# Value products behind the next pair's second score, and the second FFN pass's scale and first weights ahead of the last down products

## The chip, the cores and the metric

The kernel runs on one core of a Trainium2 chip. The core has a tensor engine for matmuls (PE, whose weight loads the profile lists as PEld), a vector engine (DVE), a scalar engine (ACT), a general engine (POOL) and a queue engine (SP, listed as SPq), each with its own queue of instructions; 16 DMA engines move data between HBM, SBUF and so on. Matmul results go to PSUM, which is used here as eight banks of 128 x 512 float32. The metric is the device time of one execution in microseconds; the time before is the median of three runs.

## The reference

One layer of a diffusion backbone on 128 context tokens and 1,024 latent tokens, nine blocks of 128 tokens (block 0 is the context), model width 1,024. Cut to what matters:

```python
h = rmsnorm(x, norm1_w) * (1 + sc1) + sh1
aq, ak, av, mq, mk, mv, mo, mg = split(h @ w_in)
attn_o = attention(aq, keys, vals)          # 8 query heads of 64, 2 key heads; 1,152 keys for latent tokens
hm = mlstm_bidir(...)                       # 4 heads of 128, chunks of 128, forward and backward
x = x + g1 * (concat([attn_o, hm]) @ w_out)
h2 = rmsnorm(x, norm2_w) * (1 + sc2) + sh2
g, u = split(h2 @ w_gu)                     # 2 x 2,816 columns
x = x + g2 * ((silu(g) * u) @ w_down)
y = rmsnorm(x, final_norm_w)
```

Everything is float32. The kernel gets that precision by splitting an operand in a high and a low part and adding three matmuls (high by high, high by low, low by high).

## The kernel before, in words

**Order.** The program is traced by Python generators that hand over to each other; a list scheduler then puts the traced instructions into the engines' queues when the kernel is built. It keeps a timeline of its own, and of the instructions that are ready on it takes the one traced first. `hot(n)` lets a block count as traced n instructions earlier. `tc.issue_after(ins)` queues what its block traces on the engine of `ins` behind `ins`: an order on that one engine, no wait for a result. On the chip each engine then works through its queue in that order. `weave(main, side, n_main, n_side)` (L66) traces `n_side / n_main` units of the side work for each unit of the main work.

**Attention** (L1087). A generator works block by block, head by head. For a head, six matmuls write the scores against all keys into S (L1128), which fills three PSUM banks and has one buffer; DVE takes the maximum (L1130), ACT the exponential (L1131), ACT and DVE make the high and low half-precision parts ph and pl (L1134, L1135), and two DMA transposes on SP's queue turn them into phT and plT (L1137, L1138), which have two buffers each, one for a pair of heads. The value products (L1152, L1153, 18 matmuls for a latent block) of a pair are a closure kept in `late`; it is traced after the second score of the next pair (L1140), or at the end of a group of three blocks (L1165). The last pair of a block is thus traced behind the second score of the next block. ACT and DVE evacuate the result (L1155, L1157). The generator is woven into three stages: beside the mLSTM heads' projections and scans (the first 560 us), beside the output projection and second norm (`prefill`), and beside the first three groups of FFN tiles.

**FFN, first pass.** Blocks 0 to 2 go through an ordinary FFN. The 22 tiles of 128 hidden columns come in five groups, GROUPS = [(0, 4), (4, 4), (8, 4), (12, 5), (17, 5)]. `gate_up` (L1476) takes for each tile a gate and an up piece of 512 KB: load into a raw tile, cast to the high part on ACT (L174), low part on DVE (L145), the sum of the absolute values on ACT (L178, kept in `wsum`), and 24 matmuls (L1472 to L1474). `down` (L1499) then takes the group's rows of w_down in two halves of 512 columns, each in three pieces for a group of five tiles (two of 512 KB, one of 256 KB), and makes 45 matmuls from them (L1214 to L1216), for block 0 first and then for blocks 1 and 2. All raw tiles of this pass come from two buffers in turn:

```python
    raw_tags = ["iraw1"]
    def raw_tile():
        loaded["raw"] = (loaded.get("raw", -1) + 1) % (2 * len(raw_tags))
        return wp.tile([P, 1024], F32, name=nm("raw"), tag=raw_tags[loaded["raw"] // 2], bufs=2)
```

**FFN, second pass.** Blocks 3 to 8 go through a scheme that needs seven products instead of eight for 2 x 2 blocks. `features6` (L1545) makes its inputs Bt while the last two groups of the first pass run: for each of six blocks two halves are transposed on PE, and for blocks 6 to 8 the sums are formed in T (L1575), a tile with one buffer (tag "S" of the pool sp). It is woven as the side work `feats`: 37 units, of which the last block's halves are units 32 and 33. `weight_scale` (L1537) takes the maximum of `wsum`, has PE transpose it (L124), brings it to a power of two on DVE (L190 to L193) and has PE broadcast it (L204). `weights6` (L1588) loads a gate and an up tile into raw tiles, forms four sums on DVE in a tile of the same tag "S" (L1597 to L1600), and for four pairs of operands the scaled high part on ACT (L1605) and the low part on DVE (L1606), in the pool a4p of seven buffers. `pair6` (L1611) calls it and makes the products (L1619 to L1621).

At the seam of the passes (L1824 to L1847) the order traced is: groups four and five whole, `feats` woven in; the rest of `feats`; `weight_scale`; the pools of the first pass closed, a third and fourth raw buffer added (L1841); then `pair6` for the first tile, which starts with `weights6`.

Of the kernel before, what the change touches and what calls it, by code (L numbers as in the profile page):

```python
# [49 lines left out]
def hybrid_step(ctx: ExitStack, tc: tile.TileContext, I: dict, O: dict):  # L50
# [24 lines left out]
    def emit(gen):  # L75
        for _ in gen:
            pass

    def chain(*gens):
        for g in gens:  # L80
            for v in g:
                yield v
# [1004 lines left out]
    def attention(c, oT, done, ha=200, hv=200, spill=None):  # L1087

        late = []
        for i in range(CB):  # L1090
            b = c * CB + i
            nk = 1 if b == 0 else NB
            with hot(ha):
                qr = ap.tile([P, NQ, HD], F32, name=nm("qr"), tag="qr", bufs=1)
                nc.scalar.dma_start(qr.rearrange("p h d -> p (h d)"), q_d[b])
                qT = ap.tile([P, NQ, P], F32R, name=nm("qT"), tag="qT", bufs=1)
                flat = qr.rearrange("p h d -> p (h d)")
                ps = bank()
                for j in range(4):
                    transpose(ps[:, j * P : (j + 1) * P], flat[:, j * P : (j + 1) * P])  # L1100
                psv = ps.rearrange("p (j x) -> p j x", j=4)
                qv = qT.rearrange("p (j g) x -> p j g x", g=2)
                for g in range(2):
                    own = slice(64 * g, 64 * g + 64)
                    far = slice(64 - 64 * g, 128 - 64 * g)
                    nc.scalar.copy(qv[own, :, g, :], psv[own])
                    sub(qv[far, :, g, :], psv[own], qv[own, :, g, :].bitcast(F32), "dve")
            yield
            for h in range(NQ):
                with hot(ha):  # L1110
                    kv = h // 4
                    if h % 2 == 0:
                        phT = ap2.tile([P, 2, NB, P], F16, name=nm("phT"), tag="phT", bufs=2)
                        plT = ap2.tile([P, 2, NB, P], F16, name=nm("plT"), tag="plT", bufs=2)
                    pr = ap2.tile([P, 3, CT], F32, name=nm("pr"), tag="pr", bufs=2)
                    ph = ap2.tile([P, 3, CT], F16, name=nm("ph"), tag="ph", bufs=2)
                    pl = ap2.tile([P, 3, CT], F16, name=nm("pl"), tag="pl", bufs=2)
                    st = ap.tile([P, 4], F32, name=nm("st"), tag="st", bufs=4)
                    if b == 0:
                        prv, phv, plv = pr[:, 0:1, 0:P], ph[:, 0:1, 0:P], pl[:, 0:1, 0:P]  # L1120
                        parts, w, c0 = 1, P, NB * P
                    else:
                        prv, phv, plv = pr, ph, pl
                        parts, w, c0 = 3, CT, 0
                    S = psum["S"].tile([P, 3, 512], F32, name=nm("S"), tag="S")
                    for n in range(parts):
                        for t in range(2):
                            mm(S[:, n, 0:w], qT[:, h, :], kst[kv][:, t, c0 + n * w : c0 + (n + 1) * w], start=(t == 0), stop=(t == 1))  # L1128
                    Sv = S[:, 0:parts, 0:w]
                    dve.tensor_reduce(out=st[:, 0:1], in_=Sv, axis=AX.XY, op=ALU.max, negate=True)  # L1130
                    act(prv, Sv, AF.Exp, bias=st[:, 0:1], accum_out=st[:, 1:2])  # L1131
                    dve.reciprocal(st[:, 2:3], st[:, 1:2])
                    dve.tensor_scalar(out=st[:, 3:4], in0=st[:, 2:3], scalar1=2.0 ** 14, scalar2=None, op0=ALU.mult)  # L1133
                    act(phv, prv, AF.Copy, scale=st[:, 3:4])  # L1134
                    dve.scalar_tensor_tensor(out=plv, in0=prv, scalar=st[:, 3:4], in1=phv, op0=ALU.mult, op1=ALU.subtract)  # L1135
                    dma_t = nc.sync.dma_start_transpose
                    dma_t(phT[:, h % 2, 0:nk, :], phv.rearrange("p a b -> p (a b)"))  # L1137
                    loaded["turned"] = dma_t(plT[:, h % 2, 0:nk, :], plv.rearrange("p a b -> p (a b)")).ins  # L1138
                yield
                if late and h % 2 == 1:  # L1140
                    late.pop()()
                    yield
                if h % 2 == 1:
                    def values(phT=phT, plT=plT, kv=kv, nk=nk, b=b, i=i, j=h // 2):
                        if j == 0:
                            oT.append(new_oT() if spill is None else ap2.tile([P, 4, P], F32, name=nm("oS"), tag="oS", bufs=1))
                        with hot(hv):
                            po = psum["po"].tile([P, 512], F32, name=nm("po"), tag="po") if "po" in psum else bank()
                            for n in range(nk):
                                vi = 9 if b == 0 else n  # L1150
                                v = vs[:, vi, kv].rearrange("p t d -> p (t d)")
                                mm(po[:, 0:256], v, phT[:, :, n, :], start=(n == 0), stop=False)  # L1152
                                mm(po[:, 0:256], v, plT[:, :, n, :], start=False, stop=(n == nk - 1))  # L1153
                            ol = ap2.tile([64, 256], F32, name=nm("ol"), tag="ol", bufs=1)
                            act(ol, po[64:128, 0:256], AF.Copy, scale=vsc[64:128, 1:2])  # L1155
                            for g in range(2):
                                dve.scalar_tensor_tensor(out=oT[i][64 * g : 64 * g + 64, j, :],  # L1157
                                                         in0=po[0:64, g * P : (g + 1) * P], scalar=vsc[0:64, 1:2],
                                                         in1=ol[:, g * P : (g + 1) * P], op0=ALU.mult, op1=ALU.add)
                        if j == 3:  # L1160
                            done.add(i)
                            if spill is not None:
                                dma(spill[i].rearrange("p (k x) -> p k x", k=4), oT[i])
                    late.append(values)
        late.pop()()  # L1165
        yield
# [443 lines left out]

    def pair6(f, Bt, acts):  # L1611

        ops = weights6(f)
        a, b, c, d = (bank()[:, 0:CT] for _ in range(4))

        def product(n, ps, first):
# [195 lines left out]
    with tc.issue_after(loaded["gate"]):  # L1812
        for _ in range(4):
# [10 lines left out]
    firsts = []  # L1824
    feats = chain(*[features6(nxt, 1, i, Bt, firsts) for i in range(CB)],
                  attn_out(far, o2, g_d[0, 1], lambda i: mixing(a4p, "A4", 7), o_d[CB:]), *[features6(far, 2, i, Bt, firsts) for i in range(CB)])
    main = groups(0, cur, GROUPS[NG:])
    weave(main, feats, 18 * sum(nf for _, nf in GROUPS[NG:]), 42)
    emit(feats)
    weight_scale()  # L1830
    es_f.close()
    es_ps.close()
    del psum["mm1"], psum["po"]
# [78 lines left out]
```

## Time and profile before

| | |
|---|---|
| median of 3 runs | 1542.33 us (1539.0 to 1546.64) |
| the profiled execution's own time | 1538.01 us |
| its span in the profile | 1536.2 us |
| mean granted PE clock | 0.97 |
| PE, DVE, ACT, POOL busy | 93%, 73%, 53%, 14% |

The profile is of one execution. Its views: a page (busy time by engine, slices, DMA, the chain of work that ended last, the costliest groups of instructions); a list of waits (who waited for whom, total us, times, longest); a timeline (start, length, engine, line, output<-inputs, and in brackets the idle time before it and what ended it); groups of instructions by line (count, busy us, mean ns, idle before); and windows (for a stretch A:B its length, then busy us and number of instructions by engine, the granted PE clock, the DMA share and GB/s; a window can be kept to one line of the kernel, and then shows that line's instructions alone). Times are from the start of the span. Matmuls overlap, so that a busy time per matmul is longer than its slot; where a number of matmuls fills a stretch, the stretch divided by the number gives the slot.

### The profile page before, as it was taken

The numbers are of one execution on the slowest core, as the hardware profiler recorded it, in microseconds if no ns is written. First come the engines' busy times: TensorE is split into PE (matmuls) and PEld (weight loads), VectorE is DVE, ScalarE is ACT, GpSimd is POOL, SyncE is SP. The second block draws the span as 40 slices with busy tenths as digits, with TensorE's granted clock in tenths as the row PEclk, the third lists the DMA queues.
The fourth block names the chain that finished last, engine by engine and source line by source line (L and its number), as shares of the span: only waits on it lengthen the run. The fifth ranks groups of instructions, "written<-read, shape, count | busy, mean of one in ns | idle before, by whom it ended". The sixth has DMA issues, their size and how long they took to land.

```text
span 1536.2 us, 22786 instructions
## 1 busy us (share of the span) xinstructions
PE 1434.6 (93%) x8281; PEld 1071.1 (70%) x8281; DVE 1126.6 (73%) x2272; ACT 810.7 (53%) x1524; POOL 222.4 (14%) x310
## 2 busy tenths in 40 slices
PE   6889899899899889999999899989999999999995
PEld 3635567676677657888989787965766667676763
DVE  4978557685777778646787766879878696886857
ACT  4855476676766745552866752844334141523233
POOL 0122332132323344510001010000000000000000
PEclk9799999999999999999999999999999999999997
DMA  9475245565449756564778733444222040412112
GB/s 371 155 227 186 68 90 96 72 150 78 81 102 158 197 187 170 145 206 138 212 177 193 185 117 117 143 132 153 81 72 94 28 137 1 138 49 76 35 35 82
DMA packets 255318, 197.02 MB, mean 128 GB/s; under 512 B 167974, under 2 KB 209142, under 8 KB 255206
## 3 DMA queue, kind: packets, MB, share of 16 engines
q1 hardware_dynamic: 252638, 191.13, 45.9%
q10 hardware_dynamic: 2440, 4.05, 1.2%
q8 instruction: 65, 1.06, 0.3%
q0 software_dynamic: 128, 0.39, 0.1%
q14 instruction: 47, 0.39, 0.1%
HBM read 143.94 MB, written 13.26 MB: 102 GB/s over the span
## 4 chain that ended last, share of the span: by engine, by line
PE 53%; DVE 4%; DMA 4%; ACT 4%; issue 1%; POOL 1%; SPq 0%; ACTq 0%; POOLq 0%
PE mm L1621 7%; PE mm L1619 7%; PE mm L1620 7%; PE mm L1687 4%; PE mm L1688 4%; PE mm L1689 4%; PE mm L1472 3%; PE mm L1474 3%; PE mm L1473 3%; PE mm L1214 2%; PE mm L1216 2%; PE mm L1215 2%; PE mm L1250 2%; DMA raw<-in_w_gu_dram 2%; PE mm L1252 2%; PE mm L1254 1%
## 5 line engine op out<-in xcount | busy, mean ns | idle before, releaser
L1619 PE MATMUL mm<-Bt,A 128*128 128x384 f16 x616 | 200.2, 328 | 1.6 <-ACT A L1605 1.6
L1620 PE MATMUL mm<-Bt,A 128*128 128x384 f16 x616 | 201.6, 327 | 0.0
L1621 PE MATMUL mm<-Bt,A 128*128 128x384 f16 x616 | 197.2, 327 | 2.4 <-DVE A L1606 2.4
L174 ACT CAST whi<-raw 128x1024 fp32r<-128x1024 f32 (+1 forms) x102 | 103.3, 1014 | 132.5 <-DMA raw<-in_w_down_dram 49.0
L145 DVE TENSOR_TENSOR wlo<-raw,whi 128x1024 fp32r<-128x1024 f32 (+1 forms) x102 | 120.7, 1183 | 53.8 <-ACT whi L174 49.0
L1135 DVE SCALAR_TENSOR_TENSOR pl<-pr,st,ph 128x1152 f16<-128x1152 f32 (+1 forms) x72 | 95.7, 1329 | 48.8 <-ACT ph L1134 45.1
L1472 PE MATMUL mm<-aTh,whi 128*128 128x384 f32 x352 | 121.7, 346 | 8.8 <-ACT ol L1155 3.1
L1474 PE MATMUL mm<-aTh,wlo 128*128 128x384 f32 x352 | 120.9, 344 | 0.8 <-DVE wlo L145 0.8
L1473 PE MATMUL mm<-aTl,whi 128*128 128x384 f32 x352 | 120.9, 343 | 0.0
L1130 DVE TENSOR_REDUCE st<-S 128x1 f32<-128x1152 f32 (+1 forms) x72 | 88.9, 1235 | 21.7 <-PE S L1128 21.2
L1131 ACT ACTIVATE pr<-S,st 128x1152 f32<-128x1152 f32 (+1 forms) x72 | 81.5, 1132 | 40.2 <-DVE st L1130 39.7
L1134 ACT ACTIVATE ph<-pr,st 128x1152 f16<-128x1152 f32 (+1 forms) x72 | 84.0, 1167 | 32.4 <-DVE st L1133 11.7
L1128 PE MATMUL S<-kst,qT 128*128 128x384 f32 (+1 forms) x400 | 89.6, 357 | 7.1 <-ACT pr L1131 7.1
L525 PE MATMUL wi<-headw,hT 128*128 128x384 f16 x288 | 94.7, 329 | 1.6 <-ACT th L815 1.4
L526 PE MATMUL wi<-headw,hT 128*128 128x384 f16 x288 | 94.6, 328 | 0.0
L527 PE MATMUL wi<-headw,hT 128*128 128x384 f16 x288 | 94.5, 328 | 0.0
L1605 ACT ACTIVATE A<-S,six 128x1024 f16<-128x1024 f32 x44 | 49.9, 1146 | 80.8 <-PE mm L1621 58.0
L1619 PEld LDWEIGHTS <-A 128*128 128x128 f16 x616 | 60.3, 98 | 44.5 <-issue 3.8
L1621 PEld LDWEIGHTS <-A 128*128 128x128 f16 x616 | 60.4, 98 | 43.2 <-DVE A L1606 3.1
L1203 DVE TENSOR_TENSOR t<-mm,hmr 128x512 f32<-128x512 f32 x84 | 54.4, 684 | 48.3 <-PE mm L1689 33.3
L1620 PEld LDWEIGHTS <-A 128*128 128x128 f16 x616 | 60.4, 98 | 39.2 <-issue 0.5
L1128 PEld LDWEIGHTS S<-kst,qT 128*128 128x128 f32 x400 | 71.0, 194 | 10.7 <-ACT pr L1131 8.4
(456 smaller groups left out, 3694.3 us busy)
## 6 DMA issues: line engine op xcount, KB each, us to landing
raw<-in_w_gu_dram SPq DMA_DIRECT2D x88, 512.0 KB
raw<-in_w_down_dram SPq DMA_DIRECT2D x40, 512.0 KB
a<-in_w_ada_dram SPq DMA_DIRECT2D x24, 512.0 KB
iraw<-in_w_in_dram SPq DMA_DIRECT2D x32, 256.0 KB
x<-in_x_sample_dram SPq DMA_DIRECT2D x11, 512.0 KB
raw<-in_w_out_dram SPq DMA_DIRECT2D x10, 512.0 KB
aw<-in_w_ada_dram SPq DMA_DIRECT2D x8, 512.0 KB
aw<-in_w_ada_dram SPq DMA_DIRECT2D x16, 256.0 KB
```

The costliest lines, as they stand in the source:

```text
L145: (dve if eng == "dve" else pool).tensor_tensor(out=out, in0=full, in1=hi, op=ALU.subtract)
L174: nc.scalar.copy(hi[:, :n], raw[:, :n])
L525: mm(ps[:, :n], ah, wh[:, k % 2, c0 : c0 + n], start=(k == 0), stop=False)
L526: mm(ps[:, :n], ah, wl[:, k % 2, c0 : c0 + n], start=False, stop=False)
L1128: mm(S[:, n, 0:w], qT[:, h, :], kst[kv][:, t, c0 + n * w : c0 + (n + 1) * w], start=(t == 0), stop=(t == 1))
L1135: dve.scalar_tensor_tensor(out=plv, in0=prv, scalar=st[:, 3:4], in1=phv, op0=ALU.mult, op1=ALU.subtract)
L1472: mm(ps, wh[:, k, :], th[:, k, :], start=(k == 0), stop=False)
L1473: mm(ps, wh[:, k, :], tl[:, k, :], start=False, stop=False)
L1474: mm(ps, wl[:, k, :], th[:, k, :], start=False, stop=(k == KD - 1))
L1619: mm(ps, wh[:, k], bt[:, 0, k], start=first and k == 0, stop=False, skip_group_check=True)
L1620: mm(ps, wh[:, k], bt[:, 1, k], start=False, stop=False, skip_group_check=True)
L1621: mm(ps, wl[:, k], bt[:, 0, k], start=False, stop=k == 3, skip_group_check=True)
```

## The change

Two edits. In the attention, the last matmul of a head's scores is kept as `score`, and the closure with the value products is traced inside `tc.issue_after(score)`: its PE instructions are queued behind the second score of the next pair, whenever they are ready. At the seam, the last group's `gate_up` and `down` are taken apart: `feats` is woven into group four and the last `gate_up` alone (150 units instead of 180), then `weight_scale` and the first tile's `weights6` are traced, and only then the last group's two halves of `down`. `pair6` takes the operands made there for tile 0. The two loads of that `weights6` and the six of these `down` now take turns in the two raw buffers in this order.

```diff
--- before.py
+++ after.py
@@ -1125,7 +1125,7 @@
                     S = psum["S"].tile([P, 3, 512], F32, name=nm("S"), tag="S")
                     for n in range(parts):
                         for t in range(2):
-                            mm(S[:, n, 0:w], qT[:, h, :], kst[kv][:, t, c0 + n * w : c0 + (n + 1) * w], start=(t == 0), stop=(t == 1))
+                            score = mm(S[:, n, 0:w], qT[:, h, :], kst[kv][:, t, c0 + n * w : c0 + (n + 1) * w], start=(t == 0), stop=(t == 1)).ins
                     Sv = S[:, 0:parts, 0:w]
                     dve.tensor_reduce(out=st[:, 0:1], in_=Sv, axis=AX.XY, op=ALU.max, negate=True)
                     act(prv, Sv, AF.Exp, bias=st[:, 0:1], accum_out=st[:, 1:2])
@@ -1138,7 +1138,8 @@
                     loaded["turned"] = dma_t(plT[:, h % 2, 0:nk, :], plv.rearrange("p a b -> p (a b)")).ins
                 yield
                 if late and h % 2 == 1:
-                    late.pop()()
+                    with tc.issue_after(score):
+                        late.pop()()
                     yield
                 if h % 2 == 1:
                     def values(phT=phT, plT=plT, kv=kv, nk=nk, b=b, i=i, j=h // 2):
@@ -1610,7 +1611,7 @@
 
     def pair6(f, Bt, acts):
 
-        ops = weights6(f)
+        ops = weights6(f) if f > 0 else first_ops
         a, b, c, d = (bank()[:, 0:CT] for _ in range(4))
 
         def product(n, ps, first):
@@ -1824,10 +1825,13 @@
     firsts = []
     feats = chain(*[features6(nxt, 1, i, Bt, firsts) for i in range(CB)],
                   attn_out(far, o2, g_d[0, 1], lambda i: mixing(a4p, "A4", 7), o_d[CB:]), *[features6(far, 2, i, Bt, firsts) for i in range(CB)])
-    main = groups(0, cur, GROUPS[NG:])
-    weave(main, feats, 18 * sum(nf for _, nf in GROUPS[NG:]), 42)
+    main = chain(groups(0, cur, GROUPS[NG:-1]), gate_up(cur, *GROUPS[-1]))
+    weave(main, feats, 18 * sum(nf for _, nf in GROUPS[NG:-1]) + 12 * GROUPS[-1][1], 42)
     emit(feats)
     weight_scale()
+    first_ops = weights6(0)
+    for n in range(2):
+        emit(down(0, cur, *GROUPS[-1], n))
     es_f.close()
     es_ps.close()
     del psum["mm1"], psum["po"]
```

## The prediction, made before the changed kernel was run

> **What bounds the kernel now.** I read the page first, then the waits of the tensor engine (PE), then PE's timeline around the two edited places, then the other queues there.
>
> ```profile
> span 1536.2 us, 22786 instructions
> PE 1434.6 (93%) x8281; PEld 1071.1 (70%) x8281; DVE 1126.6 (73%) x2272; ACT 810.7 (53%) x1524; POOL 222.4 (14%) x310
> ```
>
> PE is busy 93% of the span: the 102 us that it is not busy, and the time at half clock, are all that a reordering can win. PE's list of waits from 150 to 900 us starts with the attention:
>
> ```profile
> PE mm L1152 <- DMA phT<-ph: 7.4, 4, 3.2
> PE S L1128 <- ACT pr L1131: 7.1, 7, 2.1
> ```
>
> Value products (L1152) wait 7.4 us, four times, for transposed probabilities; scores (L1128) wait 7.1 us, seven times, for the exponential that frees their one PSUM tile. PE's timeline shows three of the first kind (the bracket is the idle time before the row and who ended it):
>
> ```profile
> 247.79 0.28 PE L1152 MATMUL mm<-phT,vs 128*128 128x256 f16 x1 [0.59 <-DMA phT<-ph]
> ```
> ```profile
> 280.76 0.28 PE L1152 MATMUL mm<-phT,vs 128*128 128x256 f16 x1 [2.09 <-DMA phT<-ph]
> 282.90 0.27 PE L1153 MATMUL mm<-plT,vs 128*128 128x256 f16 x1 [1.85 <-DMA plT<-pl]
> ```
> ```profile
> 365.07 0.27 PE L1152 MATMUL mm<-phT,vs 128*128 128x256 f16 x1 [3.21 <-DMA phT<-ph]
> ```
>
> At 280.76 a score stands queued behind the waiting value product and starts only afterwards, in half-speed matmuls:
>
> ```profile
> 283.36 2.12 PE L1128 MATMUL S<-kst,qT 128*128 128x384 f32 x6
> ```
>  The second place is the seam of the two FFN passes:
>
> ```profile
> 1024.18 0.27 PE L124 MATMUL mm<-ident,six 128*1 128x128 f32 x1
> 1026.45 0.38 PE L204 MATMUL mm<-pv,ones 1*128 1x2 f32 x2 [2.00 <-DVE pv L193]
> 1028.40 0.50 PE L1619 MATMUL mm<-Bt,A 128*128 128x384 f16 x1 [1.57 <-ACT A L1605]
> ...
> 1031.67 0.50 PE L1621 MATMUL mm<-Bt,A 128*128 128x384 f16 x1 [2.44 <-DVE A L1606]
> ```
>
> After the last down product PE does the scale's transpose, waits for its maximum, waits for the first scaled weights (ACT), then for their low parts (DVE). Stretches around such gaps (PE busy first, the granted clock sixth):
>
> ```profile
> 283.40:287.00 3.60, 3.60 (x17) 2.82 (x16) 1.45 (x3) 0.00 (x0) 0.00 (x0) 0.53 0.28 62
> 365.10:369.60 4.50, 4.50 (x25) 3.35 (x26) 0.74 (x3) 4.11 (x11) 1.62 (x4) 0.62 0.26 54
> 958.00:963.00 5.00, 2.80 (x19) 2.53 (x18) 1.74 (x4) 3.42 (x7) 0.00 (x0) 0.98 0.24 58
> 963.00:966.30 3.30, 3.30 (x13) 3.30 (x12) 2.78 (x6) 2.14 (x5) 0.00 (x0) 0.52 0.78 284
> 1005.00:1024.30 19.30, 19.30 (x85) 15.43 (x84) 11.82 (x17) 2.84 (x5) 1.02 (x1) 1.00 0.37 110
> 1027.60:1034.50 6.90, 3.66 (x12) 1.48 (x13) 5.73 (x14) 2.93 (x4) 0.00 (x0) 0.51 0.28 97
> 1034.50:1041.00 6.50, 6.50 (x42) 3.91 (x41) 6.50 (x14) 2.02 (x4) 0.00 (x0) 1.00 0.29 105
> ```
>
> After a gap of 2.2 us or more (5.00 less 2.80 at 958) some 3.4 us run at half clock, which costs 1.7 us of work.
>
> **The seam, part by part.** Before: from 1024.18 to 1034.50 pass 10.3 us. The 12 products done in them are worth 12 x 6.50/42 = 1.9 us at full clock, so 8.4 us are lost, and the second pass starts as if at 1032.6 with full clock.
>
> After: the scale and the first weights run under the last down products. Moved are one reduction, three small PE instructions, the 512 KB gate and up rows of the first tile on SP's queue, four DVE sums, four ACT scalings, four DVE low parts. What they are moved past is the six down loads, and there is the catch: all these loads take turns in two raw tiles (iraw1), so the down weights cannot be fetched until the sums and low parts have read gate and up. When does that end?
>
> ACT's last sum of absolute weights, a raw tile's load on SP's queue and the cast that it released, PE's last gate and up product, DVE's last use of the features:
>
> ```profile
> 991.80 0.19 ACT L178 ACTIVATION_READ_ACCUMULATOR jk<-raw 128x1 f32 x1
> ```
> ```profile
> 992.64 0.38 SPq L173 DMA_DIRECT2D raw<-in_w_down_dram  x1
> ```
> ```profile
> 996.94 1.05 ACT L174 CAST whi<-raw 128x1024 fp32r<-128x1024 f32 x1 [2.88 <-DMA raw<-in_w_down_dram]
> ```
> ```profile
> 1004.83 0.34 PE L1474 MATMUL mm<-aTh,wlo 128*128 128x384 f32 x1
> ```
> ```profile
> 1006.90 1.22 DVE L145 TENSOR_TENSOR Bt<-T,Bt 128x1024 f16<-128x1024 f32 x1
> ```
>
> And DVE's groups of instructions (busy us, mean ns):
>
> ```profile
> L145 DVE TENSOR_TENSOR wlo<-raw,whi 128x1024 fp32r<-128x1024 f32 x94 | 114.8, 1221 | 51.6 <-ACT whi L174 46.8 <-PE mm L204 2.1 <-PE mm L1254 1.9
> ...
> L1606 DVE SCALAR_TENSOR_TENSOR A<-S,six,A 128x1024 f16<-128x1024 f32 x44 | 56.1, 1280 | 5.3 <-ACT A L1605 5.0
> ...
> L1597 DVE TENSOR_TENSOR S<-raw 128x512 f32<-128x512 f32 x22 | 15.0, 684 | 1.0 <-DMA raw<-in_w_gu_dram 1.0
> ```
>
> The last sum of absolute weights ends at 992.0, while PE has gate and up products until 1005.2: 13 us of cover. A load takes 4.3 us (992.64 to 996.94), so the up rows, issued when that tile frees, are there at about 996.9. The scale and the first scaling together take 4.2 us now (1024.18 to 1028.40); started at 992.7 they end when the up rows land. Then DVE: four sums of 0.68 and the first low part of 1.28, 4.0 us: the gate tile is free at 1000.9. The first down piece lands at 1005.2, its cast (1.05) ends at 1006.3, its low part (1.22) at 1007.5. The up tile is free after three more low parts (two of 1.28, one of half the size, 3.2), 1004.1; the second piece is ready 6.6 us later, at 1010.7.
>
> The down products are 90; 83 stand after 1005 (85 less a gate product and a transpose), 7 ran earlier as fillers. One takes 19.30/85 = 0.227 us: 20.4 us in all. Without those fillers gate and up end 1.6 us sooner, at 1003.6. So PE idles from there to 1006.3, and again for the low part; from 1007.5 a piece is 18 products, 4.1 us: piece two is ready before PE wants it at 1011.6, and the rest, 6.6 us for a load, a cast and a low part on each of two tiles, keep up. The down products end at 1007.5 + 20.4 = 1027.9 and the second pass starts there at full clock: 1032.6 - 1027.9 = **4.7 us** won. Bounds: nothing idle, 1003.6 + 20.4 + 0.65 for the scale's PE instructions = 1024.65, 8.0 won (the second pass's first products could fill); the stall halves the clock, 1.7 less, 3.0. I take 4.7: the load's length is a row, a filler needs the scheduler to foresee the stall.
>
> Whether that stall halves the clock: in the row at 958 to 963, 2.2 us idle were enough, which puts 3.0 at the seam. The Trainium skill (TensorE: Matmul & The Clock Gate, section Why this matters for your kernels) asks only for "No PE-idle gaps >~3µs between matmul bursts"; by that the longest gap of 2.7 us would leave 4.7. The trace's 2.2 us gap speaks against the page's figure, so both values stay in the range.
>
> Behind the ACT scalings, which now wait for the scale, stand the last tile's tanh and the down casts; neither has input before gate and up end or a down piece lands. SP's queue is held by the first down load with only gate rows behind it. Features are spread over 150 instead of 180 units of the main work, so they are issued earlier:
>
> ```profile
> 955.10:981.20 26.10, 13.97 (x40) 8.09 (x40) 0.93 0.38 124
> 955.10:999.00 43.90, 24.77 (x72) 14.08 (x72) 0.96 0.40 132
> ```
>
> These count L1474 (eight a piece) in the last gate and up: a second feature half is transposed after 5 pieces, the last after 9, where the spreading puts them (units 27 and 33: 21 + 1.4 per piece). With 25.2 + 1.68 per piece, unit 33 comes at piece 5, four pieces or some 18 us earlier. The feature tile T that the four sums must wait for (one buffer, now free at 1006.90 + 1.22 = 1008.1) is then free near 990, before the up rows land.
>
> **The attention.** Order on PE only: nothing is computed twice, the evacuations (ACT L1155, DVE L1157) follow their products. Of 33 value groups that get the edge, 17 start ahead of their score now, counted in PE's timeline. These are the first and the last score that a group stands on both sides of (one earlier group, of the short context block, ends before its score):
>
> ```profile
> 237.37 1.29 PE L1128 MATMUL S<-kst,qT 128*128 128x384 f32 x6
> ...
> 865.92 1.31 PE L1128 MATMUL S<-kst,qT 128*128 128x384 f32 x6
> ```
>
> The 0.6 us at 247.79 goes. At 280.76 the score, about 1.1 us at full clock, fills part of 3.9 us, and the half clock after it (1.7) goes in half the cases: 1.9. At 365.07 the score can start only after its exponential; head products can fill the 3.2 us, and the 1.7 behind them: 0 to 4.9, I take 2.5. One group loses by it:
>
> ```profile
> 661.56 0.27 PE L1152 MATMUL po<-phT,vs 128*128 128x256 f16 x1
> 664.90 0.44 PE L1472 MATMUL mm<-aTh,whi 128*128 128x384 f32 x1 [3.06 <-ACT whi L174]
> ...
> 744.62 0.34 PE L1128 MATMUL S<-kst,qT 128*128 128x384 f32 x1
> ```
>
> Here a block's last value group runs in a stretch where PE has to wait for weights anyway. Its edge sends it behind the next block's second score, 744.62, into full PE time: some 1.4 us more: a 384-column score product takes 1.29/6 = 0.22 us, a 256-column value product two thirds of that, and I count 10 of the 18 in the wait. Attention: 0.6 + 1.9 + 2.5 - 1.4 = **3.6 us**, between -1.4 and 3.9 + 1.7 + 4.9 + 0.6 = 11.1. Transpose buffers (two) are not held longer: the values still precede the next pair's second half.
>
> Sum: 4.7 + 3.6 = 8.3 us. The profiled execution took 1538.01 us, its span 1536.2; that becomes 1529.7. The median of the runs shown is 1542.33, so **1534.0**.
>
> **The rivals.** *The attention gives its part back:* list order shifts everywhere, new waits replace the three, only the loss at 661 stays: 4.7 - 1.4, 1539.0. For it: transposes land late in other places too. Against: the stalls are named. *Scores wait instead:* what stands between a pair's scores are those values; without them PE meets scores whose exponential isn't done. Observed price 7.1/7 = 1.0 us, times 17: +17, less 4.7, 1554.6. It cancels the seam from 0.28 us a group and is slower by 0.5% from 0.73. Against: the scores at 237.37 and 865.92 show no wait, and PE has other products. *The feature tile is late:* if T still frees at 1008.1, the sums and all loads come 11.2 us later, the second pass starts at 1039.1, with halved clock 1040.8, 8.2 worse than before; with the attention's gain 1546.9. Against: the spacing above. *The edge binds nothing and the loads undo the seam:* 1542.3.
>
> **How the numbers follow.** Half a per cent (7.7 us) is about what a measurement can tell. Forecast 0.55: its own range 1.6 to 19.1 us won (3.0 - 1.4; 8.0 + 11.1), 1523 to 1541, faster 0.44, same 0.11. Attention gives back 0.16: faster 0.04, same 0.11, slower 0.01. Scores wait 0.12: same 0.01, slower 0.11. Late tile 0.12: same 0.08, slower 0.04. Nothing 0.05, same. Faster 0.48, same 0.36, slower 0.16. The range 1523 to 1549 leaves out most of the waiting scores and little else.
>
> **What would show it.** Right: no wait of L204 or L1621 at the seam, down products after a PE gap of 2 to 4 us at the end of gate and up, second-pass products at full clock from the first; the waits at 247, 281 and 365 smaller; a value group near 745 in place of 661. Wrong: L1128 waiting for L1131 in many pairs; the sums L1597 starting after 1002; PE gaps over 6 us before the last down products; or idle time that only moves to L1153.

## The result and the profile after

The kernel after took 1564.95 us (median of six runs, 1563.39 to 1568.47) beside 1541.41 us of the kernel before: a ratio of 1.0151, with a 95% interval of 1.0126 to 1.0176. The forecast was 1534.0 us in 1523 to 1549: wrong in sign, and outside its range. The profiled execution took 1564.72 us. Its page:

```profile
span 1563.0 us, 22771 instructions
PE 1436.9 (92%) x8281; PEld 1075.8 (69%) x8281; DVE 1126.7 (72%) x2272; ACT 813.4 (52%) x1524; POOL 215.8 (14%) x310
```

PE is busy 2.3 us longer (1436.9 to 1434.6); the rest of the 26.8 us is idle time, and the PE list of waits tells whose. In the kernel after, lines behind the attention's edge are one higher than before: the value products are L1153 and L1154.

```profile
PE S L1128 <- ACT pr L1131: 13.5, 10, 3.3
PE mm L1153 <- DMA phT<-ph: 7.1, 3, 3.2
PE po L1153 <- DMA phT<-ph: 7.1, 1, 7.1
PE mm L1215 <- ACT whi L174: 7.0, 1, 7.0
...
PE mm L1154 <- DMA plT<-pl: 5.5, 2, 3.6
PE mm L124 <- ACT t L1554: 5.3, 1, 5.3
```

The scores' wait for the exponential has nearly doubled (7.1 to 13.5); the value products' waits for the transposes, which the edge was to take away, are 19.7 in place of 9.8 (7.4 and 2.4), with a row of some 1 us left out on either side. Two rows point at the seam's edit: a first down product that waits 7.0 us for its weights is new, and a transpose that waits 5.3 us for the features' input waited 2.2 before.

Windows between the same PE instructions of both kernels place the loss (us):

| stretch | before | after | |
|---|---|---|---|
| heads' stage: from 190 us to a tenth of the output projection's matmuls | 369.5 | 381.8 | +12.3 |
| to group four's first gate product | 295.9 | 297.5 | +1.6 |
| to its third tile | 31.7 | 40.2 | +8.5 |
| to the last gate and up | 68.0 | 71.8 | +3.8 |
| to the end of gate and up (fewer down products inside) | 49.7 | 46.4 | -3.3 |
| to a tenth of the second pass's matmuls | 57.8 | 61.7 | +3.9 |

From there on both run alike. The sum is 26.8, the difference of the spans. For the first stretch the windows of before and of after (length, then busy us and instructions of PE, PEld, DVE, ACT and POOL, granted clock, DMA share, GB/s):

```profile
190.00:559.50 369.50, 343.19 (x2217) 252.86 (x2216) 262.68 (x621) 253.82 (x636) 112.73 (x212) 0.97 0.59 116
```
```profile
190.00:571.80 381.80, 346.11 (x2218) 254.97 (x2218) 263.12 (x622) 255.02 (x636) 106.99 (x212) 0.95 0.61 112
```

Same products; PE idle (length less busy) 35.7 against 26.3 us, 9.4 more. The value waits that should have gone stand in PE's timeline of after a little later: the pair of 281 us as large as before, the one of 365 us twice as large (6.8 us in place of 3.2):

```profile
288.28 0.28 PE L1153 MATMUL mm<-phT,vs 128*128 128x256 f16 x1 [2.11 <-DMA phT<-ph]
290.48 0.37 PE L1154 MATMUL mm<-plT,vs 128*128 128x256 f16 x1 [1.91 <-DMA plT<-pl]
...
386.68 0.28 PE L1153 MATMUL mm<-phT,vs 128*128 128x256 f16 x1 [3.19 <-DMA phT<-ph]
390.60 0.37 PE L1154 MATMUL mm<-plT,vs 128*128 128x256 f16 x1 [3.63 <-DMA plT<-pl]
...
757.49 0.28 PE L1153 MATMUL po<-phT,vs 128*128 128x256 f16 x1
```

The last row is the group of 661 us, moved behind the next block's second score as foretold. The seam after, on PE, then DVE, ACT and SP's queue:

```profile
1027.88 0.27 PE L124 MATMUL mm<-ident,six 128*1 128x128 f32 x1
1029.89 0.38 PE L204 MATMUL mm<-pv,ones 1*128 1x2 f32 x2 [1.73 <-DVE pv L193]
1037.31 1.65 PE L1215 MATMUL mm<-whi,hl 128*128 128x512 f32 x3 [7.04 <-ACT whi L174]
```
```profile
1014.35 0.19 DVE L1540 TENSOR_REDUCE six<-wsum 128x1 f32<-128x44 f32 x1
```
```profile
1030.50 1.15 ACT L1606 ACTIVATE A<-raw,six 128x1024 f16<-128x1024 f32 x1 [0.60 <-DVE six L205]
```
```profile
1032.99 5.89 SPq L173 DMA_DIRECT2D raw<-in_w_down_dram  x3
```

The maximum of the weight sums is there at 1014.54, 13.3 us ahead of the scale's transpose on PE, and that transpose comes behind the last gate and up product (1027.7). So scale, scaling, low part, raw tile, down load and cast follow one another with PE idle: the cover of 13 us existed and was not used.

### The profile page after: what moved, and what is told of

Read it like the earlier page. It is cut to its first block, busy times and chain, and to the rows that moved or that the text cites. A ratio compares the mean times of both kernels' runs of the same rounds, so it can differ in the third digit from the quotient of the medians.

```text
span 1563.0 us, 22771 instructions
## 1 busy us (share of the span) xinstructions
PE 1436.9 (92%) x8281; PEld 1075.8 (69%) x8281; DVE 1126.7 (72%) x2272; ACT 813.4 (52%) x1524; POOL 215.8 (14%) x310
## 4 chain that ended last, share of the span: by engine, by line
PE 54%; DVE 5%; ACT 4%; DMA 4%; issue 2%; POOL 1%; SPq 0%; ACTq 0%; POOLq 0%; DVEq 0%
PE mm L1620 6%; PE mm L1621 6%; PE mm L1622 6%; PE mm L1688 4%; PE mm L1689 4%; PE mm L1690 4%; PE mm L1475 3%; PE mm L1473 3%; PE mm L1474 3%; PE mm L1215 2%; PE mm L1216 2%; PE mm L1217 2%; DMA raw<-in_w_gu_dram 2%; PE S L1128 2%; PE mm L1251 1%
## 5 line engine op out<-in xcount | busy, mean ns | idle before, releaser
L1621 PE MATMUL mm<-Bt,A 128*128 128x384 f16 x616 | 200.8, 326 | 0.0
L1128 PE MATMUL S<-kst,qT 128*128 128x384 f32 (+1 forms) x400 | 88.9, 356 | 13.5 <-ACT pr L1131 13.5
L1621 PEld LDWEIGHTS <-A 128*128 128x128 f16 x616 | 60.3, 98 | 39.0
```

What stands on the lines that cost most here:

```text
L1128: score = mm(S[:, n, 0:w], qT[:, h, :], kst[kv][:, t, c0 + n * w : c0 + (n + 1) * w], start=(t == 0), stop=(t == 1)).ins
L1621: mm(ps, wh[:, k], bt[:, 1, k], start=False, stop=False, skip_group_check=True)
```

## The experiments

All runs below were on chips where the kernel before took 1534.6 to 1535.5 us, so ratios are compared; the ratio is the one on record with its interval, not the bare quotient of two medians. In the kernel before and the eleven below that leave the attention alone, the heads' stage differs in length by up to 8 us (364.2 to 372.4), nearly all of it in PE's busy time at a granted clock of 0.96 to 0.98; the idle time of PE there is 25.6 to 27.1 us.

| run | median us | ratio (95% interval) |
|---|---|---|
| edge_alone | 1545.11 | 1.0055 (1.0037 to 1.0073) |
| edge_heads | 1542.75 | 1.0045 (1.0028 to 1.0062) |
| edge_late | 1537.14 | 1.0021 (1.0006 to 1.0036) |
| edge_first | 1536.62 | 1.0002 (0.9986 to 1.0017) |
| seam_alone | 1547.65 | 1.0072 (1.0051 to 1.0093) |
| seam_oldpace | 1539.49 | 1.0029 (1.0012 to 1.0045) |
| seam_hot | 1548.51 | 1.0080 (1.0060 to 1.0101) |
| seam_po | 1549.79 | 1.0066 (1.0043 to 1.0089) |
| seam_po_hot | 1544.02 | 1.0060 (1.0040 to 1.0079) |
| seam_raws | 1541.05 | 1.0038 (1.0020 to 1.0057) |
| seam_raws_old | 1539.43 | 1.0026 (1.0010 to 1.0042) |
| seam_best | 1539.13 | 1.0013 (0.9998 to 1.0028) |
| scale_early | 1537.34 | 1.0008 (0.9991 to 1.0025) |
| turn_only | 1534.41 | 0.9993 (0.9979 to 1.0008) |
| scale_turn | 1530.74 | 0.9970 (0.9954 to 0.9985) |

My theory after the result was that each of the two edits loses by itself, and where the stretches show it; the rivals were that one of them only hands on the other's lateness, or that any change of order costs by chance.

### The attention's edge

**edge_alone**: the diff's attention part on the kernel before, nothing else.

> Only the attention's edge; the seam is as before. Theory (the loss is made where it shows, stage by stage): the profile after is 11.9 us late at the end of the heads' stage and 16.3 us late at the start of group four, all of it ahead of the seam's edit, so this kernel takes 12 to 17 us more than before, 1553 to 1558 us, with the scores' wait for the exponential near 13 us in all and the second pass starting 12 to 17 us later than before. Rival (the seam made the loss, the early lateness is absorbed by slack behind it): within 4 us of before. Prediction on record: 3.6 us less than before.

It is slower by 0.55%, 8.4 us: less than the theory's 12 to 17, which were read from one profile, and far from the forecast's gain. Its waits in the heads' stage:

```profile
PE S L1128 <- ACT pr L1131: 6.4, 5, 3.0
PE mm L1154 <- DMA plT<-pl: 5.0, 2, 3.4
PE mm L911 <- ACT kT L823: 3.7, 3, 1.3
PE mm L1153 <- DMA phT<-ph: 3.3, 2, 2.8
```

In the kernel before the same stage had 1.6 us of the first kind (three times), 2.4 of the second, 0.5 of the third and 5.9 of the fourth. So the edge won 2.6 us of the waits for high parts that it was aimed at, and paid 4.8 for scores and 2.6 for low parts; of the 3.2 more at the scan's L911, 2.2 stood at its L945 before. Idle time is 32.5 us there, 6 more than before.

**edge_heads** and **edge_late**: the edge only on the groups traced up to the end of the heads' stage, and only on those behind it (`edged` is switched where that stage ends).

```diff
-                    with tc.issue_after(score):
+                    with tc.issue_after(score) if edged[0] else nullcontext():
                         late.pop()()
```

> The edge only on the value groups that are traced beside the heads' projections and scans; the later ones and the seam are as before. Theory: the 11.9 us of the heads' stage are made there and stay: 1552 to 1555 us. Rival 1 (the lateness is absorbed behind the stage, and the losses near 890 us come from the later edges): within 4 us of before. Rival 2 (each displaced order shifts everything, so that the loss is a matter of chance): anything, with the same number of score waits and another sum.

> The edge only on the value groups traced behind the heads' stage; the seam as before. With the edge on the heads' stage alone 6.8 to 7 us over before and with all edges 8.4, this should add the difference. Theory (the price lies in the heads' stage, where scores and values alternate with the scans; behind it only the group moved out of the stall at 661 us costs, 1.4 us): 0 to 2.5 us over before, ratio 1.000 to 1.0015. Rival (the late edges cost as much per group as the early ones, some 0.4 us each for 15 groups): 5 us or more over before, ratio above 1.003.

0.45% (6.9 us) and 0.21% (3.2 us); together 0.66 beside 0.55 for all, so the prices add within the intervals. The early ones fall between the theory (11.9 us) and its first rival (under 4). The late ones cost a little more than the theory's 2.5 and less than the rival's 5, but their interval, 0.9 to 5.5 us, leaves both open. The start order of products in the traces gives the groups that each run displaces, against the kernel before: nine in the heads' stage, eight behind it. That is 0.8 and 0.4 us a group.

**edge_first**: the edge to the first score of the next pair.

```diff
+                    if h % 2 == 0:
+                        first = score
...
-                    with tc.issue_after(score):
+                    with tc.issue_after(first):
```

> The attention's edge, but to the first score of the next pair instead of the second; the seam as before. A pair's values may then stand between its two scores, under the first one's exponential. Theory (the edge to the second score takes from PE the work with which it bridged the exponential): scores' wait for the exponential falls from 12.6 us back to 7 to 9 us, and the kernel is within 0.3% of before. Rival (any fixed place for the values takes away the freedom to put them where PE is idle): the idle time of the heads' stage stays 6 us or more above before, and the kernel 0.4% or more above it.

No loss, and the heads' stage has even less idle time (365.30 less 342.45, 22.9 us):

```profile
190.00:555.30 365.30, 342.45 (x2217) 253.58 (x2217) 262.76 (x622) 253.78 (x636) 109.17 (x212) 0.96 0.60 117
```
```profile
PE mm L1155 <- DMA phT<-ph: 7.7, 3, 4.2
...
PE S L1128 <- ACT pr L1133: 2.1, 3, 0.9
```

But this edge binds little: in its trace still 17 groups that the other edge would hold back start ahead of the second score, 14 of them split around it; two that began ahead of the first score moved. So it does not show that a place under the first exponential is best. It shows that an edge as such, with the shifts of order that follow, costs nothing, which speaks against chance; the price is that of holding those 17 groups back. That the scores then wait because these values no longer bridge the exponential is read from the waits; no run gave the scores a second PSUM tile, which would test it directly.

### The seam

**seam_alone** and **seam_oldpace**: the diff's seam part on the kernel before, then the same with one number put back.

```diff
-    weave(main, feats, 18 * sum(nf for _, nf in GROUPS[NG:-1]) + 12 * GROUPS[-1][1], 42)
+    weave(main, feats, 18 * sum(nf for _, nf in GROUPS[NG:]), 42)
```

> Only the seam's edit; the attention is as before, so everything up to 867 us should be as before. Theory: +10 us over before (1549 to 1553): a stall of about 5 us for the far blocks' transposes in the second half of group four, and about 4 us more from the end of gate and up to the second pass, with one gap of about 7 us ahead of the first down product. Rival (the stalls are consequences of the attention's lateness): within 3 us of before, no gap of 5 us. Prediction on record: 4.7 us less than before.

> The seam's edit, but the features are woven in at the old pace (42 units over 180 instead of over 150); the two that are left over come behind the last gate and up. Attention as before. Theory that the faster pace makes the stall of the far blocks' transposes: that stall of about 5 us goes, 4 to 6 us less than the seam's edit alone, still 4 to 6 us more than before (1545 to 1548). Rival (the transposes come late because of their own inputs): the same as the seam's edit alone, within 2 us.

The seam's edit loses 0.72%, 11.1 us, without any edge in the attention; the rival that it inherits its stalls falls. Put back to the old pace it loses 0.29%: the pace, 150 units in place of 180, is 6.6 us of the 11. The stretches after the heads' stage, in the table's order, are 294.8, 39.1, 71.7, 47.6 and 62.9 us with the new pace and 294.7, 31.0, 67.0, 48.5 and 65.2 with the old. On the way to group four's third tile PE's list of waits has two rows with the new pace that it lacks with the old: a transpose waits 2.5 us for ACT (L178), and a gate product 2.5 us for DVE's evacuation of the features (L1563). In the next stretch, with the new pace, PE's queue has eight transposes of a far block ahead of group four's down products, and they wait for their input:

```profile
947.11 1.97 PE L124 MATMUL mm<-ident,t 128*128 128x128 f32 x8 [4.94 <-ACT t L1553]
```

At the old pace this stall is 2.20 us, as in the kernel before. What the old pace gets for that is a longer seam, since T is free late (read until 1002.60, the first sum starts at 1003.05), as one rival on record had it:

```profile
1012.15 1.65 PE L1214 MATMUL mm<-whi,hl 128*128 128x512 f32 x3 [11.99 <-ACT whi L174]
```
```profile
1007.79 16.43 SPq L173 DMA_DIRECT2D raw<-in_w_down_dram  x6
```

The first down load is issued at 1007.79, when the first weights have left the gate tile; PE had ended gate and up at 999.8.

**seam_hot, seam_po, seam_po_hot**: all with the new pace; a priority on the scale and the first weights, the value products' PSUM bank for the scale, and both.

```diff
-    weight_scale()
-    first_ops = weights6(0)
+    with hot(600):
+        weight_scale()
+        first_ops = weights6(0)
...
-        emit(power_scale(fp, ones, six[:, 7:8], six[:, 2:4]))
+        emit(power_scale(fp, ones, six[:, 7:8], six[:, 2:4], lambda: psum["po"].tile([P, 512], F32, name=nm("po"), tag="po")))
```

> The seam's edit with the new pace; the scale and the first weights are counted as traced 600 instructions earlier, so that the scheduler may put the scale's transpose among the gate and up products. Attention as before. Theory (the order of tracing keeps the scale behind the products; with the sums of absolute weights done near 1014 in the run after, 13 us ahead of the products' end, it fits under them): the gap of 7.2 us ahead of the first down product falls to under 2 us, and the kernel takes 5 to 8 us less than the seam's edit alone. Rival (the two raw tiles hold the down loads anyway): the gap stays over 4 us and the kernel within 3 us of the seam's edit alone.

> The seam's edit with the new pace; the scale's transpose and broadcast write to the PSUM bank of the attention's value products, idle by then, instead of the next bank of the FFN's ring; no priority. Attention as before. With the ring, the scale's bank is that of the last tile but one, which frees when that tile is evacuated, 3 us ahead of the products' end (1001.1 of 1004.5 in the run with the priority). Theory (bank and tracing order both hold the scale): no change alone, a gap of 6 to 7 us ahead of the first down product, within 3 us of the seam's edit alone. Rival (the bank alone holds it): the gap falls under 2 us and the second pass starts 6 to 9 us earlier than with the seam's edit alone.

> As the run with the bank of the value products, and the priority of 600 instructions on the scale and the first weights besides. Theory (bank and tracing order both hold the scale): the scale's transpose runs right behind the maximum of the sums, some 13 us ahead of the end of the gate and up products, the gap of 7 us ahead of the first down product falls under 2 us, the second pass starts 7 to 10 us earlier than with the seam's edit alone, and the kernel is within 3 us of before, since the stall of the far blocks' transposes (4 to 5 us, and half clock) stays. Rival (the raw tiles or the casts hold the down weights): a gap of 3 us or more stays there.

The priority alone moved nothing, against the theory; the bank alone neither. In the run with the priority, then in the one with both:

```profile
1004.49 0.27 PE L124 MATMUL mm<-ident,six 128*1 128x128 f32 x1
1006.50 0.38 PE L204 MATMUL mm<-pv,ones 1*128 1x2 f32 x2 [1.74 <-DVE pv L193]
1013.93 1.65 PE L1214 MATMUL mm<-whi,hl 128*128 128x512 f32 x3 [7.05 <-ACT whi L174]
```
```profile
997.63 0.27 PE L124 MATMUL po<-ident,six 128*1 128x128 f32 x1
1004.08 0.38 PE L204 MATMUL po<-pv,ones 1*128 1x2 f32 x2
...
1011.55 0.73 PE L1214 MATMUL mm<-whi,hl 128*128 128x512 f32 x2 [3.18 <-ACT whi L174]
```

With both, the transpose moves ahead of the last gate and up products and the gap falls from 7.05 to 3.18 us, not below 2, so that the rival (3 us or more) was right by its letter: the broadcast still stands 6.5 us behind its transpose. At this pace, then, order and bank hold the scale together, and the down loads behind it. This is no fixed property of the two: at the old pace, in seam_oldpace, the transpose ran at 994.98, ahead of the end of gate and up, with neither. The time is 1.0060, with an interval that overlaps that of seam_alone.

**seam_raws, seam_raws_old, seam_best**: four raw tiles from the last gate and up on, at the new pace and at the old; then, at the old pace, with the scale's bank and priority and the buffers' turns chosen.

```diff
+    def last_gate_up():
+        raw_tags.append(piece_tags.pop())
+        loaded["n"], loaded["raw"] = 3, 3
+        yield from gate_up(cur, *GROUPS[-1])
+
-    main = chain(groups(0, cur, GROUPS[NG:-1]), gate_up(cur, *GROUPS[-1]))
+    main = chain(groups(0, cur, GROUPS[NG:-1]), last_gate_up())
```

(Against the seam's edit; the later `raw_tags.append` is dropped. The line with the turns is in seam_best alone.)

> The seam's edit with the new pace; the third and fourth raw buffer are taken in from the last gate and up on, so that the first down loads do not wait for the first weights' low parts. The scale stays where it was traced. Attention as before. Theory (two causes in series: scale behind the products, then loads behind the low parts; either one removed is enough, because the down weights are then ready before the gate and up products end): the gap of 7.2 us ahead of the first down product goes, and the second pass starts 5 to 8 us earlier than with the seam's edit alone. Rival (the four rings of converted pieces, one fewer, hold the casts): a gap of 4 us or more stays, or new gaps stand in the last gate and up.

> As the run with the third and fourth raw buffer, but with the old pace of the features. There the gap ahead of the first down product was 12.0 us, with the first down load issued only when the gate tile was free. Theory (that load's wait for the raw tile is the whole gap): the gap falls under 2 us, the second pass starts some 10 us earlier than at the old pace with two buffers, and the kernel takes 4 to 8 us less than before. Rival (the feature tile T, late at this pace, holds the four sums and with them the end of the seam): the gap only moves to the start of the second pass, and the time stays within 3 us of the old pace with two buffers.

> The seam's edit with what the runs so far point to, attention as before: old pace of the features (no stall of the far blocks' transposes), the scale in the value products' bank with the priority, and the third and fourth raw buffer taken in from the last gate and up on, with the turns of raw and converted buffers set so that the first of them is not one that the down products of group four still read (that made a gap of 4.6 us at the start of the last gate and up in the two runs with more buffers). Theory (these are all the seam's causes): idle time of PE from the last gate and up to the second pass under 2 us instead of 6 to 12, the kernel 4 to 9 us less than before, 0.994 to 0.997. Rival (each gap that is closed opens another, the loads being the bound): within 3 us of before.

At the new pace the gap of 7 us ahead of the down products is gone, as the theory said, and 5 of the 11 us come back (1.0038); but a gap of 4.59 us opened at the start of the last gate and up, as the rival said. At the old pace:

```profile
958.76 0.69 PE L1472 MATMUL mm<-aTh,whi 128*128 128x384 f32 x1 [4.57 <-ACT whi L174]
...
1018.00 1.17 PE L1214 MATMUL mm<-whi,hl 128*128 128x512 f32 x3 [3.26 <-ACT whi L174]
```

With the turns set, the first of these is gone, and another stands inside the down products (PE, then SP's queue):

```profile
1014.97 1.65 PE L1214 MATMUL mm<-whi,hl 128*128 128x512 f32 x3 [6.67 <-ACT whi L174]
```
```profile
1009.28 0.34 SPq L1593 DMA_DIRECT2D raw<-in_w_gu_dram  x1
1009.88 0.33 SPq L173 DMA_DIRECT2D raw<-in_w_down_dram  x1
```

The fifth of the six down loads waited for a raw tile that the first weights held until T was free, and behind a load of the second tile. Theory lost, rival right: 1.0013. In each of these runs the first weights, ahead of the last down products, hold two of the raw tiles that the down weights need.

**scale_early, turn_only, scale_turn**: the kernel before, with the down products and first weights where they were. First the scale alone early (bank and priority); then only the turn of the raw buffers; then both.

```diff
-    weight_scale()
+    with hot(600):
+        weight_scale()
...
     raw_tags.append(piece_tags.pop())
+    loaded["raw"] = 3
```

> The kernel before with one thing of the seam's edit: the scale alone ahead of the last down products, by the means that the last runs showed to move it (the bank of the value products and a priority of 600 instructions); the down products and the first weights stay where they were. Theory (the seam's aim needs no turn of the loads: the raw tiles of the second pass's first weights are loaded under the down products already, and only the scale holds them): the waits of 2.0, 1.6 and 2.4 us for the scale and the first weights go, with the half clock behind them (1.8): 6 to 8 us less than before, ratio 0.995. Rival (the first weights stand behind other work on DVE and ACT, or their load is late): one gap of 3 to 5 us ahead of the second pass stays, ratio 0.998 to 1.000.

> The kernel before with one number changed: the turn of the raw buffers is set so that the second pass's first tile is loaded into the two old raw tiles, and its second tile into the two that were a converted piece of the last down products. With the scale early, the first weights still came at 1027.6, from loads issued only at 1023.4, when the last down products had read that piece. Theory (in the kernel before two things end the seam together, the scale at 1026.9 and the first tile's load at 1027.2): alone this takes away only what the load adds behind the scale, 0 to 3 us less than before, ratio 0.998 to 1.000; the wait of 2.0 us for the scale's maximum stays. Rival (the load is the only cause): 6 to 8 us less, ratio 0.995.

> Both: the scale early (bank of the value products, priority) and the first tile's loads in the old raw tiles; the last down products in their old place, no edge in the attention. Theory (with scale and load both under the down products nothing is left to wait for): first loads issued by 1013, scaled weights ready ahead of 1022, idle time of PE between the last gate and up and the second pass from 6 to 7 us to under 1.5, no half clock there; 6 to 8 us less than before, ratio 0.995. Rival (a third cause stands behind these, such as the statistics of the first pass's rows ahead of the scalings on ACT): a gap of 2 us or more stays.

In scale_early the scale was ready by 1005, and the seam was no shorter; the first weights came from loads issued only at 1023.43 (PE, then SP's queue):

```profile
1003.50 0.38 PE L204 MATMUL po<-pv,ones 1*128 1x2 f32 x2
1028.83 0.50 PE L1619 MATMUL mm<-Bt,A 128*128 128x384 f16 x1 [4.52 <-ACT A L1605]
1032.08 0.50 PE L1621 MATMUL mm<-Bt,A 128*128 128x384 f16 x1 [2.44 <-DVE A L1606]
```
```profile
1009.19 3.04 SPq L1593 DMA_DIRECT2D raw<-in_w_gu_dram  x2
...
1023.43 1.35 SPq L1593 DMA_DIRECT2D raw<-in_w_gu_dram  x2
```

By the buffers' turns, the first tile's rows go into the two tiles that the last down products still read as a converted piece, and the second tile's into the two free ones, loaded 14 us earlier. With the turn changed alone, the scale is what is late:

```profile
1030.30 0.38 PE L204 MATMUL mm<-pv,ones 1*128 1x2 f32 x2 [1.93 <-DVE pv L193]
1032.11 0.50 PE L1619 MATMUL mm<-Bt,A 128*128 128x384 f16 x1 [1.43 <-ACT A L1605]
```

0.9993, no change that could be told. With both, the second pass starts behind the last down product without a wait:

```profile
1001.52 0.38 PE L204 MATMUL po<-pv,ones 1*128 1x2 f32 x2
...
1022.19 0.40 PE L1216 MATMUL mm<-whi,hl 128*128 128x512 f32 x1
...
1038.84 0.40 PE L1619 MATMUL mm<-Bt,A 128*128 128x384 f16 x1 [3.30 <-DVE u L1638]
```

0.9970 (0.9954 to 0.9985), 4.6 us less than before: it beats both kernels. That this is nearly what the seam's edit was forecast to win (4.7) is a coincidence: the change is another one. Two causes ended the seam one behind the other, and either alone is worth nothing that could be told. It is short of the expected 6 to 8: a gap of 3.30 us stays, the third cause that the rival named, if not the one that it had in mind. It ends with DVE's evacuation L1638 of the first tile. DVE is busy all through the gap; ahead of that evacuation stand the second tile's low parts and the third tile's sums, and DVE had itself waited for the second tile's load, which is now the late one:

```profile
1028.26 0.69 DVE L1597 TENSOR_TENSOR S<-raw 128x512 f32<-128x512 f32 x1 [2.03 <-DMA raw<-in_w_gu_dram]
...
1035.04 1.27 DVE L1606 SCALAR_TENSOR_TENSOR A<-S,six,A 128x1024 f16<-128x1024 f32 x1
...
1038.23 0.55 DVE L1638 TENSOR_TENSOR u<-mm,u 128x384 f32<-128x384 f32 x1
```

## Why the prediction was wrong

**The seam, 4.7 us won; measured 11.1 us lost.** The step that failed first is "The last sum of absolute weights ends at 992.0, while PE has gate and up products until 1005.2: 13 us of cover". The interval was right, and after it was 13.3. But the scale needs PE twice, and I took it to be "started at 992.7" without asking where the scheduler would queue those two instructions: behind all gate and up products, which are traced earlier, and for want of a free bank. seam_hot, seam_po and seam_po_hot show that at this pace it takes both to move it. The second step that failed, and the dearer one, is the pace. I foresaw that the features come some 18 us earlier and T is free in time: so it was (T was read until 1017.27, and the sums' load released them at 1017.87). I counted what this does to PE at nothing. It cost 6.6 us (seam_alone against seam_oldpace), because earlier in the trace also means earlier in PE's queue, ahead of inputs that did not come earlier. The rival with the late T named what the old pace suffers (12.0 us at the seam). The gap ahead of the down products that I put at 2 to 4 us was 7.04. By place, in seam_alone's profile, the two stretches of group four up to its last gate and up are 11.1 us longer than before, and the two behind them 3.0.

**The account of the seam before.** Reading L204, L1619 and L1621 as the scale's waits was half of it. The load of the first weights came just as late, hidden behind the scale; scale_early shows it. An idle time's last releaser is not its only one.

**The attention, 3.6 us won; measured 8.4 lost.** The step "the 0.6 us at 247.79 goes", and the same for 280.76 and 365.07, treated three stalls as removable at their places. The waits for the high parts did shrink, by 2.6 us in the heads' stage of edge_alone; those for low parts and scores grew by 7.4. The 17 displaced groups were counted right, and the rival "scores wait instead" had the sign and the place: with the edge alone the scores' wait went from 7.1 to 12.6 us. Its price, 1.0 us a group, was double the measured 0.5 (8.4 over 17). Against it I had set scores that show no wait at 237 and 866; these were scores whose values stood ahead of them, which is the thing the edge forbids. The loss of 1.4 us for the group of 661 us was moved as said; with seven other late groups it measured 3.2.

**Both together.** 0.55 and 0.72 make 1.27%; measured 1.51 with an interval from 1.26, so that the times show no interaction. One profile hints at one: the stretch to group four's third tile, 8.5 us longer, has a wait of 7.1 us of value products for a transpose, and with either edit alone no PE gap ahead of value products there is over 1.3 us. They are the attention's last group. Its high part was made some 10 us behind the start of its score in both runs (891.21 after, 882.69 in edge_alone), but in between PE had 4.6 us of other products after and 9.1 in edge_alone. Why it had fewer stays open.

**Signs foretold.** Those for right that came: the group near 745 (757), no wait at L1621's place, second-pass products at full clock from the first. Not so: L204 still waited 1.73 us, and the waits of 281 and 365 did not shrink. Those for wrong that came: a PE gap over 6 us ahead of the down products, idle time moved to L1153, ten score waits for seven. The sums came at 1017.87, behind the 1002 that was set, but in a kernel that was 23 us late by then; in seam_alone they start at 998.17, so this sign says nothing against the features' timing.

## What to carry to other kernels

An interval on one engine is cover only for instructions that can be queued inside it: for each instruction that moves, look for the queue slot, the bank and the buffer, not only for the input. An engine's order that a scheduler left loose may be doing work; before tying it, count the instructions that are now on the other side and what they bridge. Where a wait ends, look for what would have ended it next: here two causes had to go together before anything was won.

## What the runs showed of the hardware

The length of a gap alone does not decide how the clock answers to it. The same gap of the scan (at L945, waiting for the same ACT instruction) was followed by half clock in one run and by full clock in another: seam_oldpace, then scale_turn.

```profile
403.40:405.70 2.30, 0.06 (x2) 0.04 (x1) 0.93 (x4) 2.30 (x5) 0.00 (x0) 0.91 0.47 137
405.70:408.70 3.00, 3.00 (x12) 3.00 (x13) 1.97 (x4) 2.15 (x7) 0.50 (x3) 0.50 0.00 0
```
```profile
402.70:405.00 2.30, 0.05 (x2) 0.04 (x1) 0.93 (x4) 2.30 (x5) 0.00 (x0) 1.00 0.52 137
405.00:408.40 3.40, 3.40 (x25) 3.04 (x26) 2.65 (x6) 2.79 (x10) 0.85 (x3) 1.00 0.00 0
```

After 2.24 us idle 12 products took 3.00 us at clock 0.50; after 2.25 us, 25 took 3.40 at 1.00. The Trainium skill (TensorE: Matmul & The Clock Gate, section Why this matters for your kernels) asks for no gaps over some 3 us. Here a gap of 2.2 us went either way, so the prediction's 1.7 us of lost work behind such a gap is not certain; what decided between the two was not found.
